# Keys and gates of a gated delta layer from the input without its norm factor

## Chip, core and metric

One core of a Trainium2 chip runs the whole program. The metric is the device time of one execution in microseconds (us); less is better. The kernel before took 1216.96 us, the median of three runs (1216.34 to 1221.76).

## What is computed

Two transformer blocks in a row on 256 tokens of 1024 features, in float32. The first layer is a gated delta layer; the change lies at its entrance:

```python
def rmsnorm(x, w):
    xf = x.astype(jnp.float32)
    y = xf * lax.rsqrt(jnp.mean(xf * xf, axis=-1, keepdims=True) + EPS)
    return (y * w.astype(jnp.float32)).astype(x.dtype)
...
def gated_deltanet(hn, w_in, conv_w, a_log, dt_bias, out_norm_w, w_out):
    proj = hn @ w_in
    qkv, z, b, a = jnp.split(proj, [...], axis=-1)
    qkv = jax.nn.silu(causal_dwconv(qkv, conv_w))
    q, k, v = jnp.split(qkv, [GDN_QK_DIM, 2 * GDN_QK_DIM], axis=-1)
    ...
    beta = jax.nn.sigmoid(b)
    g = -jnp.exp(a_log) * jax.nn.softplus(a + dt_bias)
    o = chunked_gated_delta_rule(q, k, v, g, beta)
    ...
```

`hn` is `rmsnorm(h, a_norm_w)`. The factor of the norm is one number for each token, the weight one for each feature, so a product with `w_in` may be taken of `h * weight` and each token's factor put on the result. q and k are then made to unit length for each head; behind this layer come its feed-forward, an attention layer, and a second block, none of which the change touches.

## The kernel before

Features lie on the 128 partitions and tokens on the free dimension: `h` is 8 tiles of 128x256. All weights come in one stream of tiles `wr` of 512 KB (128x1024, eight blocks of 128x128) in the order of use, issued on SP's queue (`_raw`, L172), four buffers deep. Each is split in two (`_prep`): ScalarE makes a rounded copy `wh` (L186), VectorE the difference `wl` (L187); each has four buffers, so a copy waits until TensorE is done with the tile four before. An input is split the same way into `xh` and `xl`, and `mm3` takes three products: `wh` with `xh`, `wh` with `xl`, `wl` with `xh` (L249 to L251). In what follows a product is one such matmul of 128x128 by 128x256, and a k-step is one of the 8 feature tiles.

`gdn` starts with warm-up products on ones (`warm`), while `h` lands in four pieces. ScalarE squares, VectorE adds the squares (`add_sq`, L502), TensorE sums over the partitions (`colsum`), a chain of short VectorE instructions makes the factor (`rstd`), and `rows` brings it into row form (a diagonal `dg` and a product with ones, `rowp`). For each k-step VectorE makes `xn` (L568), ScalarE `xh` (L569), VectorE `xl` (L570).

`gdn_body` then takes the products of `w_in`: keys (four groups of two tiles, 48 products each, the first two groups together with k outside), the gates b and a (24 products), queries (four groups), z, values. What becomes of a finished group is its evacuation: for keys and queries `conv`, which is one scaled copy on ScalarE (`cy`, L647) and three steps on VectorE (L650) for each of two tiles, then silu on ScalarE (L651) and a square (`sqg`); for the gates `evac_ba`, some fifteen short instructions on VectorE and five on ScalarE. The column sums of `sqg` (`ssb`, four products with ones, 8 records) and the gates' transposition (`bgp`) are queued some ticks later: a tick comes with every four weight blocks, that is 12 products, and steps the waiting generators (`side`). Behind the keys follow `x_stage` (kk, rp), an inverse of triangular blocks in 31 steps on VectorE (`inv_stage`), and the rest of the layer.

The program's order on each engine is set by a scheduler when it is built; each engine then works off its own queue in order. Tiles named `t2` share six buffers. `behind` fixes that one instruction stands after another without a wait.

Of the kernel before, what the change touches and what calls it, by code (L numbers as in the profile page):

```python
# [9 lines left out]
F32 = mybir.dt.float32  # L10
# [9 lines left out]
P = 128  # L20
T = 256
# [91 lines left out]
WARM = (5, 1, 3)  # L113
# [19 lines left out]
PRE0 = 1  # L133
# [5 lines left out]
PINS = {1: 0, 3: 1}  # L139
# [3 lines left out]
class Builder:  # L143
# [113 lines left out]
    def gemm(self, name, x, K, ctiles, evac, ko=0):  # L257
# [3 lines left out]
        if ko:  # L261
            banks = [self.bank() for _ in range(ko)]
            for k in range(K):
                for g in range(ko):
                    for i, c in enumerate(groups[g]):
                        wh, wl = self.w(name, k * P, c * P)
                        self.mm3(banks[g][:, i * T : i * T + T], wh, wl, xh[:, k], xl[:, k],
                                 k == 0 and i == 0, k == K - 1, True)
# [159 lines left out]
    def split(self, hi, lo, src, scale=None, eng=None):  # L428

        nc = self.nc  # L430
        if scale is None:
            nc.scalar.activation(hi, src, AF.Copy)
            nc.vector.tensor_tensor(lo, src, hi.bitcast(F32), ALU.subtract)
# [71 lines left out]
    def run(self):  # L505
        nc, tc = self.nc, self.tc
        with ExitStack() as es:
# [9 lines left out]
            self.ident = self.cp.tile([P, P], F32, name="ident")  # L517
            for b in range(4):
# [4 lines left out]
            self.ones = self.cp.tile([P, P], F32, name="ones")  # L523
            nc.gpsimd.memset(self.ones, 1.0)
# [22 lines left out]
    def gdn(self):  # L547
# [3 lines left out]
        with tc.tile_pool(name="gp", bufs=1) as gp:  # L551

            wb = self.bank("warm")
            warm = lambda n, r: [nc.tensor.matmul(wb[:, 0 : r.shape[1]], self.ones, r, start=True, stop=True) for _ in range(n)]
            warm(WARM[0], self.ones)
            for b in range(4):
                self.add_sq(self.sqs, "sqa", b, lambda o: nc.scalar.activation(o, self.h[:, 2 * b : 2 * b + 2], AF.Square))
            nc.vector.tensor_tensor(self.sqs[0], self.sqs[0], self.sqs[1], ALU.add)
            cs = self.colsum(self.sqs[:1])
            if PRE0:  # L560
                self._prep(0)
            rc = self.rstd(cs, D)
            warm(WARM[1], self.sqs[0])
            rb = self.rows(rc, psum=True)
            warm(WARM[2], self.h[:, 0])
            for i in range(8):
                t = gp.tile([P, T], F32, tag="t2", bufs=6, name="xn")
                op = nc.vector.scalar_tensor_tensor(t, self.h[:, i], self.col("a_norm", i), rb, ALU.mult, ALU.mult)  # L568
                nc.scalar.activation(x[0][:, i], t, AF.Copy)  # L569
# [1366 lines left out]
```

## Time and profile before

| what | value |
|---|---|
| median of the runs shown | 1216.96 us |
| the profiled execution | 1216.23 us |
| its span | 1214.4 us |
| TensorE (PE) busy | 1188.7 us, 98% |
| VectorE (DVE) busy | 895.2 us, 74% |
| ScalarE (ACT) busy | 687.7 us, 57% |
| GpSimd (POOL) busy | 20.4 us, 2% |
| DMA over the span | 168 GB/s read and written |

The span is the time between the first and last instruction of the profiled execution; 1.8 us lie around it. Busy shares are averages over all stages. A busy TensorE is one with products in its pipeline: products overlap, so the distance from one start to the next says what one costs. A timeline row gives the start, the length, engine, line, operation, tile and count; "idle before" in brackets is the time that the engine stood still, and what ended it. Where one row merges several instructions, its length reaches from the first start to the last end.

### The profile page before, as it was taken

The numbers are of one execution on the slowest core, as the hardware profiler recorded it, in microseconds if no ns is written. First come the engines' busy times: TensorE is split into PE (matmuls) and PEld (weight loads), VectorE is DVE, ScalarE is ACT, GpSimd is POOL, SyncE is SP. The second block draws the span as 40 slices with busy tenths as digits, with TensorE's granted clock in tenths as the row PEclk, the third lists the DMA queues.
The fourth block names the chain that finished last, engine by engine and source line by source line (L and its number), as shares of the span: only waits on it lengthen the run. The fifth ranks groups of instructions, "written<-read, shape, count | busy, mean of one in ns | idle before, by whom it ended". The sixth has DMA issues, their size and how long they took to land.

```text
span 1214.4 us, 23416 instructions
## 1 busy us (share of the span) xinstructions
PE 1188.7 (98%) x9368; PEld 1125.4 (93%) x9368; DVE 895.2 (74%) x1680; ACT 687.7 (57%) x1170; POOL 20.4 (2%) x47
## 2 busy tenths in 40 slices
PE   7999989999999999999999999999999999999997
PEld 6989878999999999889999999889789999999996
DVE  6978976668877778878977778756756567655555
ACT  5785547546655556656755556754465445444443
POOL 1000000000000000000000000000000000000000
PEclk9999999999999999999999999999999999999999
DMA  6546365355555557435555564364255563555552
GB/s 222 179 132 216 125 192 183 124 157 168 199 184 182 187 179 243 126 115 161 190 188 183 187 191 158 112 207 134 87 161 173 188 234 118 186 179 187 189 179 83
DMA packets 68318, 206.01 MB, mean 170 GB/s; under 512 B 18198, under 2 KB 18342, under 8 KB 67953
## 3 DMA queue, kind: packets, MB, share of 16 engines
q1 hardware_dynamic: 65600, 194.77, 50.3%
q0 software_dynamic: 2608, 9.75, 2.2%
q8 instruction: 73, 1.20, 0.4%
q14 instruction: 37, 0.29, 0.1%
HBM read 199.75 MB, written 4.74 MB: 168 GB/s over the span
## 4 chain that ended last, share of the span: by engine, by line
PE 92%; DVE 4%; ACT 2%; DMA 1%; issue 1%; SPq 0%; DVEq 0%; ACTq 0%
PE pb L249 21%; PE pb L250 20%; PE pb L251 20%; PE acc L249 7%; PE acc L250 7%; PE acc L251 7%; DVE wl L187 1%; PE pt L1138 1%; PE ssb L669 1%; DMA wr<-wall 0%; DMA h<-xT 0%; PE z2p L855 0%; PE y2p L847 0%; PE kv L1542 0%; PE csum L366 0%
## 5 line engine op out<-in xcount | busy, mean ns | idle before, releaser
L187 DVE TENSOR_TENSOR wl<-wr,wh 128x1024 fp32r<-128x1024 f32 x362 | 441.5, 1223 | 193.7 <-ACT wh L186 192.3
L186 ACT ACTIVATE wh<-wr 128x1024 fp32r<-128x1024 f32 x362 | 381.6, 1057 | 338.3 <-issue 101.1
L251 PE MATMUL pb<-xh,wl 128*128 128x256 f32 x1224 | 345.6, 283 | 3.9 <-DVE wl L187 3.9
L249 PE MATMUL pb<-xh,wh 128*128 128x256 f32 x1224 | 347.8, 284 | 0.6 <-ACT xh L569 0.6
L250 PE MATMUL pb<-xl,wh 128*128 128x256 f32 x1224 | 345.5, 282 | 0.2 <-DVE xl L570 0.2
L249 PEld LDWEIGHTS pb<-xh,wh 128*128 128x128 f32 x1224 | 231.7, 189 | 2.8 <-issue 1.3
L251 PEld LDWEIGHTS pb<-xh,wl 128*128 128x128 f32 x1224 | 229.7, 188 | 4.5 <-DVE wl L187 4.5
L250 PEld LDWEIGHTS pb<-xl,wh 128*128 128x128 f32 x1224 | 230.1, 188 | 0.5 <-DVE xl L570 0.4
L249 PE MATMUL pb<-fh,wh 128*128 128x256 f32 x416 | 118.3, 285 | 0.0
L250 PE MATMUL pb<-fl,wh 128*128 128x256 f32 x416 | 117.5, 283 | 0.1
L251 PE MATMUL pb<-fh,wl 128*128 128x256 f32 x416 | 116.6, 281 | 0.0
L249 PE MATMUL acc<-ah,wh 128*128 128x256 f32 x352 | 98.7, 280 | 0.0
L251 PE MATMUL acc<-ah,wl 128*128 128x256 f32 x352 | 98.5, 280 | 0.0
L250 PE MATMUL acc<-al,wh 128*128 128x256 f32 x352 | 98.5, 280 | 0.0
L249 PEld LDWEIGHTS pb<-fh,wh 128*128 128x128 f32 x416 | 77.9, 188 | 1.4 <-issue 0.4
L250 PEld LDWEIGHTS pb<-fl,wh 128*128 128x128 f32 x416 | 78.1, 188 | 1.1 <-DVE fl L436 0.3
L251 PEld LDWEIGHTS pb<-fh,wl 128*128 128x128 f32 x416 | 78.9, 190 | 0.0
L977 DVE SCALAR_TENSOR_TENSOR fy<-fpad,cols,fy 128x256 f32<-128x256 f32 x176 | 73.6, 478 | 0.0
L249 PE MATMUL pb<-wh,xh 128*128 128x512 f32 (+1 forms) x176 | 70.5, 402 | 0.0
L250 PE MATMUL pb<-wl,xh 128*128 128x512 f32 (+1 forms) x176 | 68.1, 387 | 0.5 <-DVE wl L187 0.5
L251 PE MATMUL pb<-wh,xl 128*128 128x512 f32 (+1 forms) x176 | 68.0, 387 | 0.0
L249 PEld LDWEIGHTS acc<-ah,wh 128*128 128x128 f32 x352 | 66.9, 190 | 0.0
(437 smaller groups left out, 2091.2 us busy)
## 6 DMA issues: line engine op xcount, KB each, us to landing
wr<-wall SPq DMA_DIRECT2D x362, 512.0 KB, 3.6
wzd<-zt POOLq DMA_DIRECT2D x8, 256.0 KB, 3.0
wzog<-wzd POOLq DMA_DIRECT2D x4, 512.0 KB, 5.2
bias<-bd POOLq DMA_DIRECT2D x4, 512.0 KB, 7.7
h<-xT SPq DMA_DIRECT2D x4, 256.0 KB, 4.0
h<-xT POOLq DMA_DIRECT2D x1, 1024.0 KB, 5.9
wrow<-wrow POOLq DMA_DIRECT2D x1, 1024.0 KB, 10.0
out_dram<-mw SPq DMA_DIRECT2D x4, 256.0 KB, 2.0
```

The source lines that it names most:

```text
L186: nc.scalar.activation(hi, r, AF.Copy)
L187: i = nc.vector.tensor_tensor(lo, r, hi.bitcast(F32), ALU.subtract)
L249: mm(out, ah, bh, start=start, stop=False, skip_group_check=skip)
L250: mm(out, ah, bl, start=False, stop=False, skip_group_check=skip)
L251: mm(out, al, bh, start=False, stop=stop, skip_group_check=skip)
L669: nc.tensor.matmul(ssb[:, c : c + 1], sq[:, i, tt * P : tt * P + P], self.ones[:, 0:1], start=True, stop=True)
L977: nc.vector.scalar_tensor_tensor(y[:, i], u[:, i, j : j + T], w(j), y[:, i], ALU.mult, ALU.add)
L1138: nc.tensor.transpose(pt[:, j * P : j * P + P], S[:, i, j * P : j * P + P], self.ident)
```

## The change

Raw input: `rawtile` makes `rawh` (ScalarE, `h` times the norm's weight) and `rawl` (VectorE) for each k-step, without the factor. Keys and gates take their products of these; each key group is multiplied by the factor's row form in a new step `ku` (VectorE, out of PSUM) before its convolution, and the gates in one of 48x256. Queries, z and values still take normed x, which is now made in a generator (`norm`): GpSimd multiplies `ha` (`h` times the weight, made by GpSimd too) by the row form, ScalarE rounds, GpSimd makes the difference. GpSimd adds the squares; the column sum is queued 7 ticks in, the row form 4 ticks after it, and is copied to SBUF (`rowb`). SP's queue takes pieces of `h` and weight tiles by turns, `ident` goes to GpSimd's queue, and the norm's weight (`anw`) has a small DMA of its own on ScalarE's. The warm-up is 13 products. The first two key groups' products come in three runs for each k-step. The gates' transposition waits nine ticks, not six. Two small products of weights for the last block (`wfp`, `w1f`) are put behind the last split of the feed-forward.

```diff
-WARM = (5, 1, 3)
+WARM = 13
+NA1, NA2 = 7, 4
...
@@ gemm, the first ko groups
+                for o, wh, wl, first in ts:
+                    mm(o, wh, xh[:, k], start=first, stop=False, skip_group_check=True)
+                for o, wh, wl, first in ts:
+                    mm(o, wh, xl[:, k], start=False, stop=False, skip_group_check=True)
+                for o, wh, wl, first in ts:
+                    mm(o, wl, xh[:, k], start=False, stop=k == K - 1, skip_group_check=True)
...
@@ run
+            nc.scalar.dma_start(self.anw, self.a["cols"][:, 0:KD])
             for b in range(4):
                 nc.sync.dma_start(self.h[:, 2 * b : 2 * b + 2], self.a["xT"][:, 2 * b : 2 * b + 2])
-            nc.sync.dma_start(self.ident, self.cst("ident"))
-            self._raw(0)
+                if b < 3:
+                    self._raw(b)
+            nc.gpsimd.dma_start(self.ident, self.cst("ident"))
             nc.sync.dma_start(self.cols, self.a["cols"])
...
@@ gdn
+            def rawtile(i):
+                act.append(nc.scalar.activation(raw[0][:, i], self.h[:, i], AF.Copy, scale=self.anw[:, i : i + 1]))
+                dve.append(nc.vector.scalar_tensor_tensor(raw[1][:, i], self.h[:, i], self.anw[:, i : i + 1], raw[0][:, i].bitcast(F32), ALU.mult, ALU.subtract))
...
+            nc.gpsimd.tensor_tensor(s0, s0, s1_, ALU.add)
...
+            nc.gpsimd.tensor_tensor(s0, s0, s2_, ALU.add)
...
+            fold = nc.gpsimd.tensor_tensor(s0[:, 0], s0[:, 0], s0[:, 1], ALU.add)
+            dve.append(nc.vector.tensor_tensor(s3_[:, 0], s3_[:, 0], s3_[:, 1], ALU.add))
...
+            def norm():
+                for _ in range(NA1):
+                    yield
+                rc = self.rstd(self.colsum([s0[:, 0], s3_[:, 0]]), D)
+                for _ in range(NA2):
+                    yield
+                self.rb = self.rows(rc)
+                self.ready = True
+                self.flush()
+                for i in range(8):
+                    t = gp.tile([P, T], F32, tag="t2", bufs=6, name="xn")
+                    nc.gpsimd.tensor_tensor(t, self.ha[i], self.rb, ALU.mult)
+                    nc.scalar.activation(x[0][:, i], t, AF.Copy)
+                    nc.gpsimd.tensor_tensor(x[1][:, i], t, x[0][:, i].bitcast(F32), ALU.subtract)
+                    yield
...
@@ evac_ba
+            nc.vector.tensor_tensor(e1[A], b[A, :T], self.rb[A], ALU.mult)
...
             def later():
-                for _ in range(6):
+                for _ in range(9):
                     yield
...
@@ mk_evac
+                if key == "kss":
+                    u = t2([P, 2, T], "ku")
+                    nc.vector.tensor_tensor(u, ev2(b), self.bc2(self.rb), ALU.mult)
+                    b = u.rearrange("p a t -> p (a t)")
                 conv(b, ct0 + 2 * g, d)
...
-        gk = self.gemm("w_in", x, KD, list(range(8, 16)), mk_evac(kT, 0, 8, "kss"), ko=2)
+        gk = self.gemm("w_in", raw, KD, list(range(8, 16)), mk_evac(kT, 0, 8, "kss"), ko=2)
         next(gk)
-        list(self.gemm("w_ba", x, KD, [0], evac_ba))
+        list(self.gemm("w_ba", raw, KD, [0], evac_ba))
```

Three places of the order. ScalarE from the last copies of x to the first key group, before (L569 makes `xh`, L186 a weight copy `wh`, L647 the convolution's first step `cy`, L613 to L617 are the gates):

```order
L569 ACTIVATE xh<-xn 128x256 x3
L186 ACTIVATE wh_306<-wr_244 128x1024
L186 ACTIVATE wh_349<-wr_274 128x1024
L647 ACTIVATE cy<-pb,cols 128x256
L186 ACTIVATE wh_410<-wr_304 128x1024
L186 ACTIVATE wh_440<-wr_347 128x1024
L647 ACTIVATE cy<-pb,cols 128x256
L613 ACTIVATE gcr<-gr 16x256
L615 ACTIVATE gr<-gr 48x256
L647 ACTIVATE cy<-pb,cols 128x256
L617 ACT_TABLE_LOAD
L617 ACTIVATE gr<-gr 48x256
```

ScalarE from the end of the first key group's convolution to the first copies `xh` in the changed kernel (L185 is the weight copy, L714 is `cy`, L718 silu, L680 to L684 the gates, L732 the square, L630 makes `xh`):

```order
L718 ACT_TABLE_LOAD
L718 ACTIVATE kT<-cy 128x512
L680 ACTIVATE gcr<-gr 16x256
L732 ACTIVATE sqg<-kT 128x512
L682 ACT_TABLE_LOAD
L682 ACTIVATE gr<-gr 48x256
L714 ACTIVATE cy<-ku,cols 128x256
L684 ACT_TABLE_LOAD
L684 ACTIVATE gr<-gr 48x256
L714 ACTIVATE cy<-ku,cols 128x256
L630 ACTIVATE xh<-xn 128x256 x2
L185 ACTIVATE wh_602<-wr_509 128x1024
```

All copies of x stood ahead of the first `cy` before; now the first key group with its silu and square, all of the gates, the second group's `cy` and three table loads stand ahead of the first `xh`.

GpSimd from its last memset of the start to its cast of the mask, before:

```order
L1009 MEMSET w1f 128x16
L589 CAST identb<-ident 128x128
L584 DMA mask_186<-cst 128x384
L767 MEMSET h 32x32x32
L588 CAST mask3b<-mask_186 128x384
```

and in the changed kernel, to the first differences `xl` (L602 to L610 add squares, L638 makes `ha`, L629 `xn`, L631 `xl`):

```order
L1080 MEMSET w1f 128x16
L655 CAST identb<-ident 128x128
L602 ISA
L602 TENSOR_TENSOR sq<-sq 128x512
L605 TENSOR_TENSOR sq<-sq 128x512
L610 TENSOR_TENSOR sq<-sq 128x256
L638 TENSOR_TENSOR ha<-h,anw 128x256 x8
L650 DMA mask_172<-cst 128x384
L838 MEMSET h 32x32x32
L654 CAST mask3b<-mask_172 128x384
L629 TENSOR_TENSOR xn<-ha,rowb 128x256 x2
L631 TENSOR_TENSOR xl<-xn,xh 128x256 x2
```

Eleven instructions on two inputs each, with an ISA instruction in front, stand ahead of the mask, and `xn` and `xl`, which were VectorE's, behind it.

TensorE in the changed kernel, from the queries' second k-step on, with the gates' transposition (L702) and an `ssb` (L740); `wh_511` and `wh_602` are the first and the third weight tile of the queries:

```order
L248 MATMUL pb<-xh,wh_511 128x256
L249 MATMUL pb<-xl,wh_511 128x256
L250 MATMUL pb<-xh,wl_512 128x256
L248 MATMUL pb<-xh,wh_511 128x256
L702 MATMUL bgp<-ident,stk 128x80 x2
L249 MATMUL pb<-xl,wh_511 128x256
L250 MATMUL pb<-xh,wl_512 128x256
L248 MATMUL pb<-xh,wh_602 128x256
L249 MATMUL pb<-xl,wh_602 128x256
L250 MATMUL pb<-xh,wl_603 128x256
L248 MATMUL pb<-xh,wh_602 128x256
L249 MATMUL pb<-xl,wh_602 128x256
```

Before, the queries' first tile was done as a whole, and the second after it; now the first tile stops behind its third k-step, and the first three k-steps of the second tile stand in between.

## Rows read from the trace of the kernel before

**Rows 1.** The page's first part: busy time, share of the span, instructions.

```profile
PE 1188.7 (98%) x9368; PEld 1125.4 (93%) x9368; DVE 895.2 (74%) x1680; ACT 687.7 (57%) x1170; POOL 20.4 (2%) x47
```

**Rows 2.** Stretches: length, busy time (instructions) of each engine, clock, DMA share, GB/s.

```profile
15.00:30.00 15.00, 14.11 (x113) 13.71 (x114) 12.48 (x21) 7.62 (x13) 2.25 (x3) 1.00 0.52 172
...
120.00:160.00 40.00, 37.50 (x258) 33.97 (x256) 39.63 (x100) 22.01 (x37) 0.00 (x0) 1.00 0.49 150
160.00:200.00 40.00, 37.22 (x447) 33.29 (x448) 24.96 (x51) 21.96 (x45) 2.14 (x4) 1.00 0.62 198
```

**Rows 3.** TensorE in time: start, length, what [idle before].

```profile
0.99 2.50 PE L554 MATMUL warm<-ones 128*128 128x128 f32 x10 [0.99 <-POOL ones L524]
9.29 1.01 PE L366 MATMUL csum<-ones,sqa 128*128 128x1 f32 x4 [5.80 <-DVE sqa L558]
...
13.26 0.74 PE L418 MATMUL rowp<-dg,ones 128*128 128x128 f32 x4 [0.19 <-DVE dg L416]
...
15.02 0.50 PE L249 MATMUL pb<-xh,wh 128*128 128x256 f32 x2 [0.59 <-ACT xh L569]
...
42.12 0.29 PE L251 MATMUL pb<-xh,wl 128*128 128x256 f32 x1
42.24 0.95 PE L669 MATMUL ssb<-ones,sqg 128*128 128x1 f32 x8
43.05 0.36 PE L249 MATMUL pb<-xh,wh 128*128 128x256 f32 x1
...
56.80 0.39 PE L249 MATMUL pb<-wh,xh 128*128 128x512 f32 x1
```

**Rows 4.** ScalarE in time, the first 13 us.

```profile
4.11 0.63 ACT L557 ACTIVATE sqa<-h 128x512 f32<-128x512 f32 x1 [2.10 <-DMA h<-xT]
...
8.43 1.06 ACT L186 ACTIVATE wh<-wr 128x1024 fp32r<-128x1024 f32 x1 [1.23 <-DMA wr<-wall]
...
10.45 1.06 ACT L186 ACTIVATE wh<-wr 128x1024 fp32r<-128x1024 f32 x1 [0.74 <-DMA wr<-wall]
11.73 1.06 ACT L186 ACTIVATE wh<-wr 128x1024 fp32r<-128x1024 f32 x1 [0.23 <-DMA wr<-wall]
```

**Rows 5.** ScalarE in time, the first key group.

```profile
34.13 1.28 ACT L617 ACT_TABLE_LOAD   x1
...
38.11 0.63 ACT L651 ACTIVATE kT<-cy 128x512 f32<-128x512 f32 x1
38.65 0.45 ACT L647 ACTIVATE cy<-pb,cols 128x256 f32<-128x256 f32 x1
39.00 0.62 ACT L661 ACTIVATE sqg<-kT 128x512 f32<-128x512 f32 x1
```

**Rows 6.** VectorE in time, gates and convolution.

```profile
32.33 0.53 DVE L611 TENSOR_SCALAR gr<-pb,cols 48x256 f32<-48x256 f32 x1
...
36.13 0.40 DVE L618 SCALAR_TENSOR_TENSOR gr<-gr 48x256 f32<-48x256 f32 x1
...
40.89 0.55 DVE L626 TENSOR_TENSOR gch<-gcr,gch 16x384 fp32r<-16x384 f32 x1
41.47 2.43 DVE L650 SCALAR_TENSOR_TENSOR cy<-pb,cols,cy 128x255 f32<-128x255 f32 x6
```

**Rows 7.** VectorE by form (280 to 400 us); two of its lines, ns min/median/max; GpSimd's cast.

```profile
L970 DVE TENSOR_TENSOR fpad<-pb,rowb 128x512 f32<-128x512 f32 x15 | 10.2, 688 | 4.6 <-PE pb L251 4.6
...
L570 DVE TENSOR_TENSOR xl<-xn,xh x8: 412/416/721, 15.2 to 21.0; 128x256 fp32r<-128x256 f32 x8
...
L187 DVE TENSOR_TENSOR wl<-wr,wh x362: 1202/1225/1520, 10.7 to 1198.2; 128x1024 fp32r<-128x1024 f32 x181
...
21.08 0.66 POOL L588 CAST mask3b<-mask 128x384 bf16<-128x384 f32 x1
```

**Rows 8.** TensorE's last product, and the stretch of the end.

```profile
1206.46 0.39 PE L251 MATMUL acc<-wh,al 128*128 128x512 f32 x1
...
1212.00:1214.00 2.00, 0.00 (x0) 0.00 (x0) 0.00 (x0) 0.00 (x0) 0.00 (x0) 0.50 0.37 142
```

More of the change, by code (lines that the diff above doesn't have):

```diff
@@ L132 @@
 PTD = (1, 3)
-PRE0 = 1
 NX = 2
@@ L138 @@
 QS = "sgss"
-PINS = {1: 0, 3: 1}
 ORDER = "qqzqqzvvvvvvzvvz"
@@ L553, in gdn @@
             wb = self.bank("warm")
[L554 to L561, printed above, removed]
@@ L574, in gdn @@
-            self.gdn_body(gp, x)
-    def gdn_body(self, gp, x):
+            for _ in range(WARM):
+                nc.tensor.matmul(wb[:, 0:P], self.ones, self.ones, start=True, stop=True)
+            raw = (gp.tile([P, KD, T], F32R, tag="XA", name="rawh"), gp.tile([P, KD, T], F32R, tag="EA", name="rawl"))
+            act, dve = [], []
+            act.append(nc.scalar.activation(self.sp.tile([P, 2], F32, tag="rky", bufs=2, name="tl"), self.ones[:, 0:2], AF.Square))
+            def rawtile(i):
+                act.append(nc.scalar.activation(raw[0][:, i], self.h[:, i], AF.Copy, scale=self.anw[:, i : i + 1]))
+                dve.append(nc.vector.scalar_tensor_tensor(raw[1][:, i], self.h[:, i], self.anw[:, i : i + 1], raw[0][:, i].bitcast(F32), ALU.mult, ALU.subtract))
@@ new lines, in part, with square @@
+            def part(j, s):
+                r, hi, lo = self.raws0[j], *self.halves[j]
+                act.append(nc.scalar.activation(hi[:, s], r[:, s], AF.Copy))
+                dve.append(nc.vector.tensor_tensor(lo[:, s], r[:, s], hi[:, s].bitcast(F32), ALU.subtract))
+            def square(b):
+                t = gp.tile([P, 2, T], F32, tag="t2", bufs=6, name="sq")
+                act.append(nc.scalar.activation(t, self.h[:, 2 * b : 2 * b + 2], AF.Square))
+                return t
+            self.raws0 = {}
@@ new lines, in gdn @@
+            for j in range(3):
+                self.raws0[j] = self.raws.pop(j)
+                self.raws[j] = None
+                self.halves[j] = (self.wtile(j, F32R, "wh"), self.wtile(j, F32R, "wl"))
+            lo, hi, full = slice(0, 512), slice(512, 1024), slice(0, 1024)
+            rawtile(0)
+            part(0, lo)
+            rawtile(1)
+            part(0, hi)
+            rawtile(2)
+            rawtile(3)
+            part(1, full)
+            s0 = square(0)
+            rawtile(4)
@@ new lines, in gdn @@
+            rawtile(5)
+            s1_ = square(1)
+            self._raw(3)
+            nc.gpsimd.tensor_tensor(s0, s0, s1_, ALU.add)
+            part(2, full)
+            s2_ = square(2)
+            nc.gpsimd.tensor_tensor(s0, s0, s2_, ALU.add)
+            rawtile(6)
+            rawtile(7)
+            s3_ = square(3)
+            self._raw(4)
+            fold = nc.gpsimd.tensor_tensor(s0[:, 0], s0[:, 0], s0[:, 1], ALU.add)
+            dve.append(nc.vector.tensor_tensor(s3_[:, 0], s3_[:, 0], s3_[:, 1], ALU.add))
@@ new lines, in gdn @@
+            for l in (act, dve):
+                for p, n in zip(l, l[1:]):
+                    self.behind(n, p)
+            self.dvl = dve[-1]
+            self.ready = False
+            def norm():
[13 more added lines that the diff above has]
+                    yield
@@ L577, in gdn_body @@
+            hab = gp.tile([P, KD, T], F32, tag="vn", name="ha")
+            self.ha = [hab[:, i] for i in range(8)]
+            for i in range(8):
+                self.behind(nc.gpsimd.tensor_tensor(self.ha[i], self.h[:, i], self.anw[:, i : i + 1].to_broadcast([P, T]), ALU.mult), fold)
+            self.side(norm())
+            self.gdn_body(gp, x, raw)
+    def gdn_body(self, gp, x, raw):
         nc, tc, sp = self.nc, self.tc, self.sp
@@ L589, in gdn_body @@
         nc.gpsimd.tensor_copy(identb, self.ident)
-        nc.vector.tensor_tensor(identr, self.ident[:, 32:48], self.ident[:, 64:80], ALU.add)
+        self.behind(nc.vector.tensor_tensor(identr, self.ident[:, 32:48], self.ident[:, 64:80], ALU.add), self.dvl)
         stk = gp.tile([P, T], F32, tag="stk", name="stk")
```

30 lines of the change are left out of this document (10 added, 20 removed).

## Prediction

> **What bounds the kernel now.** I read the page's first part, then the stretches, then TensorE in order of time. The first part says who is the limit: TensorE is busy 1188.7 of 1214.4 us, VectorE comes next with 74% [rows 1]. A saving is worth only what it lets TensorE start earlier or not wait. The stretches say where it waits: 0.89 us in 15 to 30, 2.5 in 120 to 160, where VectorE is busy 39.63 of 40, 2.8 in 160 to 200 [rows 2]. TensorE's own rows show the largest hole: the first real product stands at 15.02 us; ahead of it are only warm-up products, the column sum and the row form [rows 3]. From there a product of 256 columns follows the last after 0.12 us (42.12 to 42.24). My landmark is the first product of z, 56.80 us. Ahead of it stand 312 products of keys, gates and two groups of queries (counted in the order; the same 312 in both programs), three groups of ssb (0.81 us each, 42.24 to 43.05) and the gates' transposition: 15.02 + 312 x 0.12 + 3 x 0.81 + 0.2 = 55.1 us, and 1.7 us of waits. What the change gives must be seen there.
>
> **The start.** The raw products need one piece of h and half a weight tile. h's first piece landed at 4.11 us. The first tile is now second on SP's queue, not sixth; tiles of 512 KB that were waited for came 1.28 us apart (10.45, 11.73), so it lands at 5.4 to 5.8; its half is copied in 0.63 us, as a Square of 512 columns [rows 4]. TensorE could start at 6.2. The 13 warm-up products are 26 records, where 10 took 2.50 us: at that pace they end at 7.5, at rowp's (4 in 0.74) at 5.8 [rows 3]. I take 6.5 and keep 6.2 and 7.5. ScalarE and VectorE now scale h, split the first tiles and square in turn; from their queues TensorE waits about 0.5 us in the first four tiles. The second square is done at about 11.2 (second tile copied by 9.4, then two squares and two scalings), the fourth tile's copy at 15.3.
>
> Into TensorE's stream come the column sum (8 records as in ssb, 0.81) and the row form (0.74) [rows 3]. Had nothing else to wait, z would start at 6.5 + 37.4 + 2.6 + 0.8 + 0.7 + 0.5 = 48.5: **8.3 us earlier.**
>
> **What is late next: x for the queries.** They still take normed x, and its making starts behind the row form, 141 products in. Before, the factor took from 10.30 (end of the column sum) to 13.26 with one weight difference inside [rows 3]; now three are inside, 5.4 us from 17.9: ready in time. The row form ends at 6.5 + 16.9 + 0.8 + 0.5 + 0.7 = 25.4, and TensorE reaches the first product with x 75 products later, at 34.4. ScalarE's queue (the order above) puts all of the first key group and of the gates ahead of the first xh. Start to start:
> - rowb 0.4: 25.9. VectorE: ku 0.69 (as the feed-forward's product with rowb), the gates' product 0.53, a weight difference 1.23, six convolution steps 2.43 [rows 6, 7]: 30.7.
> - ScalarE waits for that: table load 1.28, kT 0.54, tanh 0.4, sqg 0.6, table load 1.28, exponential 0.4, cy 0.36, table load 1.28, logarithm 0.4, cy 0.36 (the short ones priced as cy) [rows 5]: 37.5. The first xh ends at 37.9. TensorE has waited **3.5 us**.
> - VectorE waits for the logarithm (37.1), then makes the gates' rows. Before, these took from 36.13 to 41.44, first to last, with one weight difference and two convolution steps among them [rows 6]; with four steps and no difference it is 4.9 us: 42.0. Then ku, a step, and the difference that the second query tile needs: 44.3, some 2.5 us after TensorE has used the three k-steps of x that it had.
> - ScalarE again: table load, kT, cy, sqg from 43.1: 45.9; only then xh 3 to 6, at 0.36 each. GpSimd makes each one's xl. No row has a GpSimd instruction with two inputs; the nearest is the cast of 128x384 in 0.66 us [rows 7], 1.7 ns an element: 0.44 for 256 elements, 0.88 for the 512 read. I take the middle, 0.66. The four end at 48.9. Then 11 products of the second tile, ssb and the eighth k-step: 51.3; 51 products are left, 6.1 us. Two halves of a step overlap with the products, 0.3: z starts at **57.1, against 56.80.** The 8.3 us are used up on one chain through ScalarE and VectorE.
>
> **VectorE and GpSimd.** GpSimd was busy 20.4 us in all [rows 1]; it gets 11 instructions early (two of 512 columns), 16 later. Does that cost VectorE? The rows say yes: the cast (21.08 to 21.74) fell on an xl of 0.721 where the median is 0.416 and on a weight difference of 1.520 where it is 1.225: 0.6 us lost for 0.66 [rows 7]. Early, 13 x 0.66 = 8.6 us from 11.2 on lie over the difference of the fourth tile, which is due at 16.6 (80 products): I count 1.0 us of TensorE's waiting. Later, five instructions, 3.3 us, fall on the gates' rows: I count 1.5. Each could be 0, were VectorE idle or elsewhere.
>
> GpSimd's first sum has an ISA instruction in front that the old order lacks there. It has no row; the nearest load is a table's 1.28 us [rows 5], and I allow 0 to four times that. It can start at some 6.5 us, when ident is cast; until 11.2 the squares hide it, and 2 us more the slack of the sum, which is due at 17.1. I take 0. The GPSIMD Engine Reference of the Trainium skill (Instruction dispatch) gives about 6 us for the first call after a load; by it the sum stays as it is.
>
> **At nothing.** ident goes to GpSimd's queue and cols behind three tiles on SP's; the first reader of ident is GpSimd's cast, and cols stands ahead of the fourth tile, which is needed later than the third. The gates' transposition stands 22 products later in TensorE's order; its reader, the keys' factors, waits for the last ssb anyway. The products of the first two key groups in three runs a k-step: the same count. wfp and w1f behind the last split: two short instructions in a stretch where VectorE isn't the limit; ahead of the boundary they would cost under 0.5. 16 xn and xl leave VectorE, 8 raw differences and 4 ku come: ahead of z it is a limit only on the chain above. After z's start TensorE's order is the old one, so its offset there is carried to the end; VectorE has then one convolution (2.43) more before it, which is free if it is idle for so long before the inverse begins, and otherwise lies in the range.
>
> **The sum.** +0.3 + 1.0 + 1.5 = +2.8 us on the profiled execution's 1216.23: **1219.0**. The median of the runs shown is 0.73 above that execution; I leave the number there. With each step's bounds (start -0.3 and +1.0, GpSimd's price -1 and +2.5, the chain's other terms -2 and +2, both contentions 0): 1213 to 1224.
>
> **Rivals.**
> - *x in time (faster).* If the chain to xh is shorter than I add up, TensorE keeps the 8.3 us less the early contention: 1216.2 - 8.3 + 1.0 = 1209. It is decided at TensorE's first query product: from there a k-step of x must come every 1.4 us. For it: I add every step at its full price. Against it: three table loads stand ahead of xh, in an order that is fixed. 0.19.
> - *VectorE and GpSimd exclude each other (slower).* If each instruction of the one with two inputs in SBUF waits for a whole one of the other, they go in turn. The fourth weight difference, which has three other differences, a sum and identr ahead of it, then starts at 19.1, not 15.3, and ends at 20.3: 3.7 us of TensorE's time. Later, five xn and xl on the gates' rows cost 3.3, and three xl that each stand behind a weight difference or convolution steps 3: 0.3 + 3.7 + 6.3 = +10.3, **1226**. For it: 0.6 lost of 0.66. Against: many of VectorE's instructions there have one input, or one in PSUM. It decides once the fourth difference starts after 17 us. 0.28. The page SBUF — State Buffer of the Trainium skill (SBUF: two separate sides) says just this for two SBUF inputs against a GpSimd instruction that reads SBUF, "an exclusive lock, not a bandwidth split"; the cast's row agrees, but no row has long runs of both.
> - *The start isn't early.* If SP's pieces land together and not in turn, the first tile lands as before (copied from 8.43 on [rows 4]) and products start at 9.2: +2.7, 1222. The 1.28 us speak against it. 0.04, within no change.
> - TensorE's clock: it ended at 1206.85, and the granted clock read 0.50, the lower level, in 1212 to 1214 [rows 8]. In 34 to 51 us TensorE works less than half the time. At the lower level the last 51 products would take 6.1 us more at most; I take 0 and put 3 into the range.
>
> **How the numbers follow.** 0.5%, 6.1 us, is about what a measurement of this kernel can tell from no change: faster is below 1210.9, slower above 1223.0. Forecast 0.49 (its own range 1213 to 1224), late start 0.04, x in time 0.19, exclusion 0.28. So faster 0.19, no change 0.53, slower 0.28. The range takes in most of both sides: 1210 to 1229.
>
> **What will show it.** Right: the first raw product at 6.2 to 7.5 us; a wait of TensorE for ScalarE's xh at about 34, another for a weight difference some 8 us later; z's first product at 57 to 60. x in time would put that at 49 to 51. Exclusion would show as GpSimd rows of 128x256 over 1 us, weight differences over 1.6, and over 2 us of waiting for the fourth. I am wrong if z starts early and the end doesn't follow, or if TensorE waits in 120 to 200 us for much more than the 5.3 us of before.

## The result, and the profile after

The changed kernel takes 1226.65 us (median of 5 runs, 1226.09 to 1228.79), the kernel before 1218.74 in the runs taken with it: a ratio of 1.0077, 95% interval 1.0062 to 1.0092. It is 0.8% slower, by 7.9 us in the medians and by 10.0 in the two profiled executions (1226.25 against 1216.23). The forecast was 1219.0, with a range to 1229.

First the page's first part (before: [rows 1]). GpSimd's 28.8 us more have not made VectorE idler: it is busy 9.0 us longer, and ScalarE 6.4.

```profile
PE 1196.2 (98%) x9380; PEld 1132.2 (92%) x9380; DVE 904.2 (74%) x1675; ACT 694.1 (57%) x1183; POOL 49.2 (4%) x75
```

TensorE in order of time (before: [rows 3]; start, length, in brackets the idle time before and what ended it).

```profile
0.99 5.24 PE L564 MATMUL warm<-ones 128*128 128x128 f32 x26 [0.99 <-POOL ones L525]
6.81 0.74 PE L270 MATMUL pb<-rawh,wh 128*128 128x256 f32 x4 [0.58 <-ACT wh L576]
...
18.49 0.74 PE L274 MATMUL pb<-rawh,wl 128*128 128x256 f32 x4 [1.58 <-DVE wl L186]
...
36.27 0.28 PE L250 MATMUL pb<-rawh,wl 128*128 128x256 f32 x1
39.98 0.58 PE L248 MATMUL pb<-xh,wh 128*128 128x256 f32 x1 [3.44 <-ACT xh L630]
40.36 1.70 PE L740 MATMUL ssb<-ones,sqg 128*128 128x1 f32 x8
...
44.78 0.50 PE L702 MATMUL bgp<-ident,stk 80*128 80x80 f32 x2 [1.23 <-issue]
...
48.75 0.58 PE L250 MATMUL pb<-xh,wl 128*128 128x256 f32 x1 [2.53 <-DVE wl L186]
...
58.28 0.48 PE L248 MATMUL pb<-xh,wh 128*128 128x256 f32 x2
58.74 0.39 PE L249 MATMUL pb<-xl,wh 128*128 128x256 f32 x1
...
65.08 0.39 PE L248 MATMUL pb<-wh,xh 128*128 128x512 f32 x1
...
172.45 0.24 PE L894 MATMUL y1p<-h,XA 32*32 32x32 f32 x2
```

The last of these rows in the kernel before:

```profile
164.35 0.24 PE L823 MATMUL y1p<-h,XA 32*32 32x32 f32 x2
```

The raw products start 8.2 us earlier, the first product of z 8.3 later. Between them TensorE waits 1.6 for the fourth weight difference, 3.4 for the first xh, 1.2 for the gates' transposition, 2.5 for a weight difference of the queries. From z on the offset is carried: 8.10 at the first product of the inverse's stage (y1p, 172.45 against 164.35), 10.09 at the last product (1216.55 against 1206.46, [rows 8]).

ScalarE's queue shows where x stands (before: [rows 5]).

```profile
27.58 0.38 ACT L428 ACTIVATE rowb<-rowp 128x256 f32<-128x256 f32 x1 [1.56 <-PE rowp L424]
...
39.53 0.71 ACT L630 ACTIVATE xh<-xn 128x256 fp32r<-128x256 f32 x2
...
47.20 0.51 ACT L714 ACTIVATE cy<-ku,cols 128x256 f32<-128x256 f32 x1 [3.46 <-DVE ku L728]
47.73 1.28 ACT L718 ACT_TABLE_LOAD   x1
...
50.48 1.32 ACT L630 ACTIVATE xh<-xn 128x256 fp32r<-128x256 f32 x4
54.87 0.51 ACT L714 ACTIVATE cy<-ku,cols 128x256 f32<-128x256 f32 x1 [3.07 <-DVE ku L728]
...
57.22 0.40 ACT L630 ACTIVATE xh<-xn 128x256 fp32r<-128x256 f32 x1
```

Four xh stand behind the second key group, the eighth behind the third, and the third and the fourth key group each begin with a wait for VectorE's ku. The last xl ends at 58.69. TensorE takes it up at 58.74, after a wait of some 0.2 us, and z follows 6.4 us after the xl, the time of the products that still stand ahead of it.

VectorE beside GpSimd, by form (28 to 62 us; in all, mean ns of one, idle before), and GpSimd's two groups:

```profile
L717 DVE SCALAR_TENSOR_TENSOR cy<-ku,cols,cy 128x253 f32<-128x253 f32 x8 | 5.5, 695 | 0.1
L717 DVE SCALAR_TENSOR_TENSOR cy<-ku,cols,cy 128x255 f32<-128x255 f32 x8 | 4.7, 598 | 1.8 <-ACT cy L714 1.8
L717 DVE SCALAR_TENSOR_TENSOR cy<-ku,cols,cy 128x254 f32<-128x254 f32 x8 | 4.7, 595 | 0.1
...
L691 DVE COPY gcr<-gcr 16x128 f32<-16x128 f32 x1 | 0.8, 768 | 0.0
...
L629 POOL TENSOR_TENSOR xn<-ha,rowb 128x256 f32<-128x256 f32 x8 | 9.4, 1175 | 7.1 <-DVE cy L717 4.8 <-DVE gch L693 1.8 <-ACT kT L718 0.5
L631 POOL TENSOR_TENSOR xl<-xn,xh 128x256 fp32r<-128x256 f32 x8 | 6.7, 857 | 7.2 <-ACT xh L630 7.2
```

One of the same rows in the kernel before (14 to 58 us):

```profile
L650 DVE SCALAR_TENSOR_TENSOR cy<-pb,cols,cy 128x255 f32<-128x255 f32 x10 | 4.7, 474 | 0.4 <-ACT cy L647 0.3
```

The 24 convolution steps of the keys take 14.9 us, each counted at its own length; at the 0.47 of before they would take 11.3. Last, stretches (length, busy time and instructions of each engine, granted clock): TensorE's clock falls to 0.50, the lower level, while it waits.

```profile
36.00:42.00 6.00, 2.56 (x15) 2.35 (x13) 3.13 (x6) 5.14 (x9) 1.99 (x3) 0.79 0.12 47
42.00:54.00 12.00, 8.22 (x36) 7.37 (x36) 11.84 (x18) 5.93 (x11) 8.59 (x10) 0.50 0.27 86
54.00:58.00 4.00, 4.00 (x24) 3.76 (x23) 3.96 (x9) 2.36 (x5) 1.75 (x3) 0.68 0.02 6
```

### The profile page after: what moved, and what is told of

It is laid out like the page before. It is cut to its first block, busy times and chain, and to the rows that moved or that the text cites. A ratio compares the mean times of both kernels' runs of the same rounds, so it can differ in the third digit from the quotient of the medians.

```text
span 1224.5 us, 23491 instructions
## 1 busy us (share of the span) xinstructions
PE 1196.2 (98%) x9380; PEld 1132.2 (92%) x9380; DVE 904.2 (74%) x1675; ACT 694.1 (57%) x1183; POOL 49.2 (4%) x75
## 4 chain that ended last, share of the span: by engine, by line
PE 88%; DVE 7%; ACT 3%; issue 1%; DMA 0%; DVEq 0%; SPq 0%; ACTq 0%
PE pb L248 19%; PE pb L249 19%; PE pb L250 18%; PE acc L248 7%; PE acc L249 7%; PE acc L250 7%; DVE wl L186 2%; DVE cy L717 1%; PE pb L274 1%; PE pb L270 1%; PE pb L272 1%; PE ssb L740 1%; DMA wr<-wall 0%; ACT wh L185 0%; PE z2p L926 0%
## 5 line engine op out<-in xcount | busy, mean ns | idle before, releaser
L186 DVE TENSOR_TENSOR wl<-wr,wh 128x1024 fp32r<-128x1024 f32 x359 | 438.8, 1225 | 190.3 <-ACT wh L185 188.8
L185 ACT ACTIVATE wh<-wr 128x1024 fp32r<-128x1024 f32 x359 | 378.9, 1057 | 332.0 <-issue 97.5
L250 PE MATMUL pb<-xh,wl 128*128 128x256 f32 x1072 | 305.7, 285 | 5.6 <-DVE wl L186 5.6
L248 PE MATMUL pb<-xh,wh 128*128 128x256 f32 x1072 | 307.1, 287 | 3.4 <-ACT xh L630 3.4
L249 PE MATMUL pb<-xl,wh 128*128 128x256 f32 x1072 | 305.3, 285 | 0.0
L248 PEld LDWEIGHTS pb<-xh,wh 128*128 128x128 f32 x1072 | 205.4, 192 | 5.4 <-ACT xh L630 3.6
L250 PEld LDWEIGHTS pb<-xh,wl 128*128 128x128 f32 x1072 | 203.7, 190 | 6.4 <-DVE wl L186 6.3
L249 PEld LDWEIGHTS pb<-xl,wh 128*128 128x128 f32 x1072 | 204.1, 190 | 0.4 <-POOL xl L631 0.2
```

Of the source, the lines that this page charges most:

```text
L185: nc.scalar.activation(hi, r, AF.Copy)
L186: i = nc.vector.tensor_tensor(lo, r, hi.bitcast(F32), ALU.subtract)
L248: mm(out, ah, bh, start=start, stop=False, skip_group_check=skip)
L249: mm(out, ah, bl, start=False, stop=False, skip_group_check=skip)
L250: mm(out, al, bh, start=False, stop=stop, skip_group_check=skip)
```

## The experiments

Each edit is made to the changed kernel. Ratios are to the kernel before on the same chip. Theory A: VectorE and GpSimd get in each other's way, and that is the loss. B: TensorE's lower clock is. C: x comes late in ScalarE's order. D and E, from the first runs: the end is set by VectorE's work behind the row form, whatever TensorE does.

### GpSimd's late half of x on VectorE (e1_late_v)

```diff
-nc.gpsimd.tensor_tensor(t, self.ha[i], self.rb, ALU.mult)
+nc.vector.tensor_tensor(t, self.ha[i], self.rb, ALU.mult)
-nc.gpsimd.tensor_tensor(x[1][:, i], t, x[0][:, i].bitcast(F32), ALU.subtract)
+nc.vector.tensor_tensor(x[1][:, i], t, x[0][:, i].bitcast(F32), ALU.subtract)
```

> The sixteen xn and xl of the changed kernel are made on VectorE instead of GpSimd, in the same place of the program, nothing else. Theory A (VectorE and GpSimd get in each other's way, and that is most of the loss): GpSimd's rows of 0.73 to 0.99 us become VectorE rows of 0.42, the convolution steps beside them go back from 0.48-0.59 to 0.41, the gates' rows take 5 us rather than 6.8, the last xl ends at about 54 rather than at 57.7, z starts at about 62 rather than 65.1: 1223.5. Theory C (the order in which ScalarE takes keys, gates and x is what holds TensorE, whoever makes x): x comes when ScalarE's queue lets it, z stays at 64 to 66: 1225 to 1228. Theory B (TensorE's lower clock is the loss): no change, 1226.5.

Measured: 1227.35, ratio 1.0079 (1.0066 to 1.0092), z at 66.29. VectorE, the same view:

```profile
L717 DVE SCALAR_TENSOR_TENSOR cy<-ku,cols,cy 128x255 f32<-128x255 f32 x8 | 3.6, 478 | 1.7 <-ACT cy L714 1.7
...
L631 DVE TENSOR_TENSOR xl<-xn,xh 128x256 fp32r<-128x256 f32 x8 | 3.2, 418 | 0.5 <-ACT xh L630 0.5
L629 DVE TENSOR_TENSOR xn<-ha,rowb 128x256 f32<-128x256 f32 x8 | 3.0, 414 | 0.0
...
L691 DVE COPY gcr<-gcr 16x128 f32<-16x128 f32 x1 | 0.2, 217 | 0.0
```

The rows do what theory A says: a convolution step goes from 0.60 to 0.70 back to 0.48, the copy from 0.77 to 0.22. In all 4.1 us come back on the 24 steps (14.9 to 10.8) and 2.4 on six stretched instructions of the gates: 6.5. But the sixteen instructions cost VectorE 6.2. It is a swap at par, and theory A's 1223.5 is a miss. The last xl ends at 58.57, where it ended at 58.69. That z is 1.2 later even so is TensorE's: from 52.5 to 59.6 it has no wait, but its clock reads 0.50 and a product comes every 0.21 us.

### h times anw on ScalarE (e2_ha_act)

```diff
-self.behind(nc.gpsimd.tensor_tensor(self.ha[i], self.h[:, i], self.anw[:, i : i + 1].to_broadcast([P, T]), ALU.mult), fold)
+self.behind(nc.scalar.activation(self.ha[i], self.h[:, i], AF.Copy, scale=self.anw[:, i : i + 1]), self.whs[3 + n])
```

(two of the eight behind each of the fourth to seventh weight copies)

> The eight products h times anw are made on ScalarE behind the weight copies instead of on GpSimd, so GpSimd runs only the three sums early; late xn and xl stay on GpSimd. Theory A: the fourth weight difference starts at 15.5 rather than 17.2 and takes 1.23, TensorE's wait for it (1.6) goes, the last raw product stands at about 34.5 rather than 36.3, rowb at 25.7 rather than 27.6, and everything behind it is 2 us earlier: z at 63, 1224.5. Theory C: the same 1.6 to 2 us, as only the early part is touched, but the wait for xh stays at 3.4. Theory B: z within 0.5 of 65.1, 1226.5.

Measured: 1224.89, ratio 1.0067 (1.0048 to 1.0085). TensorE's wait for the fourth difference is 0.73, not 1.58, rowb starts at 26.59, not 27.58; the wait for xh is still 3.43, z is at 64.53. The early contention is worth 1.0 us at the row form; its effect on the whole time is within the intervals.

### Idle products in the waits (e3_warm)

```diff
+FILL = {(0, 0, 0): 15, (0, 0, 2): 8, (0, 0, 3): 12}
...
+        for _ in range(n):
+            i = self.nc.tensor.matmul(o, self.ones, self.ones, start=True, stop=True, skip_group_check=True)
```

(numbers of idle products ahead of the first, third and fourth k-step of the first query group; some fall on sums already open in that bank, so the queries' values change, the instructions don't)

> 35 idle products of 128x128 are put into TensorE's order where it waits (15 ahead of the first query product, 8 ahead of the third k-step, 12 ahead of the fourth), written to columns that a later product overwrites. The granted clock should then stay near 1.0 from 36 to 54 us, where it fell to 0.50. Theory B (the clock is the loss): the last 48 query products and the ssb groups run at 0.12 and 0.9 us rather than 0.21 and 1.7, z starts 3 to 4 us earlier, at 61.5: 1223. Theories A and C: the last xl comes at 57.7 all the same, z stays within 0.8 of 65.1: 1226 to 1227.

Measured: 1226.50, ratio 1.0072 (1.0059 to 1.0085). The same stretches as above:

```profile
36.00:42.00 6.00, 5.36 (x42) 4.77 (x42) 3.20 (x6) 5.08 (x9) 2.06 (x3) 1.00 0.07 27
42.00:54.00 12.00, 9.87 (x76) 9.08 (x74) 11.84 (x18) 5.93 (x11) 8.60 (x10) 0.93 0.27 88
54.00:58.00 4.00, 4.00 (x19) 3.85 (x19) 3.96 (x9) 2.37 (x5) 1.75 (x3) 0.50 0.01 5
```

and the product that corresponds to the one at 58.28 above:

```profile
59.50 0.49 PE L258 MATMUL pb<-xh,wh 128*128 128x256 f32 x2
```

The clock is up at 1.00 and 0.93 until 54, and z stands at 66.06, 0.2 beyond what A and C allowed and not earlier; the last xl ends at 58.63, as without. As z needs 6.4 us from the last xl on, no clock could have brought it ahead of 65.0 here: as the cause of this kernel's late z, theory B falls. But the run does not show that the lower clock is free. From 52.5 on products come every 0.21 us again, after another wait of 1.5 us for sqg, and TensorE reaches the eighth k-step only 0.9 us after its xl has landed. In the changed kernel it was there some 0.2 us ahead of it. So x and the clock hold z at nearly the same time, and a version that brings x earlier meets the clock next.

### x ahead of keys and gates, on VectorE (e6_xfirst_v)

```diff
-                self.ready = True
-                self.flush()
                 for i in range(8):
...
-                    nc.gpsimd.tensor_tensor(t, self.ha[i], self.rb, ALU.mult)
+                    nc.vector.scalar_tensor_tensor(t, self.h[:, i], self.anw[:, i : i + 1], self.rb, ALU.mult, ALU.mult)
...
-                    nc.gpsimd.tensor_tensor(x[1][:, i], t, x[0][:, i].bitcast(F32), ALU.subtract)
-                    yield
+                    nc.vector.tensor_tensor(x[1][:, i], t, x[0][:, i].bitcast(F32), ALU.subtract)
+                self.ready = True
+                self.flush()
...
-                self.behind(nc.gpsimd.tensor_tensor(self.ha[i], self.h[:, i], self.anw[:, i : i + 1].to_broadcast([P, T]), ALU.mult), fold)
```

> x comes first: the evacuations of keys and gates are held until all eight k-steps of x are queued, and xn and xl are made on VectorE straight from h, anw and the row form (no ha, nothing late on GpSimd). Theory C (the order on ScalarE): rowb at 26 to 27.6, then 16 VectorE instructions of 0.42: the last xl by 35, before TensorE ends the raw products at 34.5 to 36.4; no wait for xh; z at 36.4 + 96 x 0.12 + 2.6 + 0.3 = 50.8 if the keys' late evacuation holds nothing, 53 if it costs a wait of 2: 1212 to 1215, faster than before by 3 to 6. Theory A: only what the two engines cost each other comes back, 1.6 early and 3 late: z at 60, 1222. Theory B: whatever shortens the waits keeps the clock up; it adds at most the 3 to 4 of the idle-product run to either.

Measured: 1224.14, ratio 1.0059 (1.0040 to 1.0077). TensorE:

```profile
47.99 0.50 PE L697 MATMUL bgp<-ident,stk 80*128 80x80 f32 x2 [5.68 <-issue]
...
57.40 0.40 PE L248 MATMUL pb<-wh,xh 128*128 128x512 f32 x1
```

No wait for x at all, as theory C has it; but the gates, now behind x, make TensorE wait 5.7 us for their transposition, and from 48 to 54 its clock reads 0.51. Theory C's z (50.8 to 53) and time (1212 to 1215) are misses. z comes 0.6 later than before, and y1p 7.4 later (171.80; the profiled execution took 1227.22, and its clock read 0.96 from 120 to 160 us, so that part of the 7.4 may be the execution's). So z was no landmark for the end any more: theories D and E.

### x for free (e5_x_free)

```diff
-raw = (gp.tile([P, KD, T], F32R, tag="XA", name="rawh"), gp.tile([P, KD, T], F32R, tag="EA", name="rawl"))
+raw = x
...
-                    nc.gpsimd.tensor_tensor(t, self.ha[i], self.rb, ALU.mult)
-                    nc.scalar.activation(x[0][:, i], t, AF.Copy)
-                    nc.gpsimd.tensor_tensor(x[1][:, i], t, x[0][:, i].bitcast(F32), ALU.subtract)
...
-                self.behind(nc.gpsimd.tensor_tensor(self.ha[i], self.h[:, i], self.anw[:, i : i + 1].to_broadcast([P, T]), ALU.mult), fold)
```

> Queries, values and z take the raw halves too: norm factor, xn, xh and xl are left out altogether, so the output lacks the factor there. It prices the chain that makes x. Theory C (x comes late on ScalarE and VectorE, and z starts 6.4 after the last xl): no wait for xh; TensorE next waits for the gates' transposition, which is 2 to 4 earlier without x in the queues: z at 52 to 56, 1214 to 1217. Theory D (the end is set behind z, by VectorE's queue up to the end of the inverse; in the x-first run z was 0.6 late and the end 11): z early, but y1p no earlier than 170 and the end at 1222 or more.

Measured: 1218.85 (10 runs, 1214.49 to 1223.04), ratio 1.0001 (0.9984 to 1.0018). (Some products of z now stand ahead of queries, so z is no mark here.) TensorE waits 2.7 us at the first row form of the gates (46.38), until VectorE's ku; y1p is at 165.61, 1.3 behind the kernel before, in a profiled execution of 1222.99. Making x (ha with it) costs the change all of its loss, and without it the 8.2 us of early start still buy nothing. Both theories miss: the time lies between C's 1214 to 1217 and D's 1222, and y1p does not stand at D's 170. Where the early start goes is in the trace. First the stretch from the end of rowb to the first product of the keys' decay, and one of TensorE behind its waits (third busy time: VectorE; then the clock):

```profile
26.96:71.61 44.65, 41.53 (x267) 38.70 (x265) 34.16 (x80) 33.07 (x52) 0.00 (x0) 0.89 0.37 125
```

```profile
48.90:57.80 8.90, 8.90 (x42) 8.90 (x43) 7.35 (x13) 2.59 (x4) 0.00 (x0) 0.50 0.70 233
```

and VectorE's longest waits in the first:

```profile
56.57 1.23 DVE L186 TENSOR_TENSOR wl<-wr,wh 128x1024 fp32r<-128x1024 f32 x1 [1.55 <-ACT wh L185]
60.78 2.43 DVE L706 SCALAR_TENSOR_TENSOR cy<-pb,cols,cy 128x255 f32<-128x255 f32 x6 [2.98 <-ACT cy L703]
66.33 1.23 DVE L186 TENSOR_TENSOR wl<-wr,wh 128x1024 fp32r<-128x1024 f32 x1 [1.81 <-ACT wh L185]
```

VectorE is busy 34 of 44.7 us here and stands idle for 6.3 between 54.9 and 66.3, so its work is not what bounds this stretch. TensorE waits 3.1 (2.7, then 0.4 for sqg) and then runs without a wait at the lower clock, where 35 products come every 0.21 us and not every 0.12 and an ssb takes 1.56 and not 0.81: by these rows I estimate 4 us. The two are 7 of the 8.2. A run with x for free and the clock kept up was not made, so what the early start would then be worth stays open.

### x first, and the transposition later (e9_xfirst_gates_late)

```diff
 (the run with x first, and)
-                for _ in range(9):
+                for _ in range(24):
```

> The x-first run with one number more: the gates' transposition is queued 24 ticks behind the gates instead of 9, so 328 products stand ahead of it, not 264, and it lies just behind the start of z. Theory C: the wait of 5.7 for it goes, TensorE reaches z at 51 to 52 without a wait: 5 earlier than before. If TensorE's early start carried through, the end would be at 1212 to 1214. Theory D: the keys' factors and the inverse come no earlier for it, the wait moves behind z (the keys' products and row forms wait for gates and keys), y1p at 170 to 172 as in the x-first run: 1222 to 1225.

Measured: 1230.20, ratio 1.0094 (1.0078 to 1.0110).

```profile
47.99 0.39 PE L248 MATMUL pb<-wh,xh 128*128 128x512 f32 x1
...
182.96 0.24 PE L889 MATMUL y1p<-h,XA 32*32 32x32 f32 x2
```

z starts 8.8 us **earlier** than before, and the inverse's first product 18.6 **later**. The transposition, queued behind 328 products, comes only at 58.93, and VectorE copies its result at 75.31, behind four weight differences; the keys' decay comes at 81.40. It isn't the only thing that is late: TensorE also waits 3.5 us for sqg, and its clock reads 0.50 from 54 to 62 and 0.65 from 62 to 70. Neither theory's time holds (D's 1222 to 1225 is a miss too). An early z alone is worth nothing here.

### The row form early (e7_row_early, e8_row_early_ha)

```diff
-NA1, NA2 = 7, 4
+NA1, NA2 = 6, 1
```

(both; in the second h times anw is on ScalarE too, behind the fifth weight copy)

> Two numbers only: the column sum one tick and the row form four ticks earlier in TensorE's order (72 and 96 products ahead of them instead of 84 and 141). Theory C: rowb is made at 22 to 23 rather than 27.6 (the factor, 2.6 us of VectorE plus two weight differences behind the column sum, is the limit), the whole chain of keys, gates and x moves with it, last xl at 53.5, z at 60: 1221 to 1222. Theory D: z at 60 as well, but as VectorE has the same work up to the inverse, y1p comes 1 to 2 earlier at most: 1224 to 1225. Theory A (the two engines in each other's way): sums and ha now lie beside the factor's instructions, rowb not before 25, z at 62 or later: 1224.

> The row form early as in the run above, and h times anw on ScalarE instead of GpSimd. Theory C: rowb at 21 to 22, the fourth weight difference not held (raw phase ends at 35 rather than 36.4), the xh stand between keys and gates in ScalarE's order: z at 56 to 58, the clock stays up for more of it: 1216 to 1219, level with before. Theory D: z at 56 to 58, end at 1222 or more.

Measured: 1230.83, ratio 1.0098 (1.0084 to 1.0113), and 1227.56, ratio 1.0070 (1.0057 to 1.0084). The row form in the first and in the second:

```profile
25.62 1.23 PE L424 MATMUL rowp<-dg,ones 128*128 128x128 f32 x4 [4.99 <-DVE dg L422]
```

```profile
21.84 0.71 PE L425 MATMUL rowp<-dg,ones 128*128 128x128 f32 x4 [1.64 <-DVE dg L423]
```

With ha on GpSimd the factor is not made sooner, and TensorE waits 5.0 for it (theory A's 25, at z 69.57); without, the row form is 3.8 earlier. Even so z is only at 64.47: x, now earlier on GpSimd, falls on the keys' convolution, whose first six steps take 3.91 where they take 2.45 in the run with x first. The first run's expected times were all too low; of the second's only theory D's "1222 or more" holds.

### The row form early, nothing late on GpSimd (e10_row_early_v)

```diff
-NA1, NA2 = 7, 4
+NA1, NA2 = 6, 2
```

(with xn and xl on VectorE as in the run with x first, in their old place, and no ha)

> Nothing late on GpSimd and no ha: xn and xl on VectorE from h, anw and the row form, x in its old place between the keys; column sum one tick and row form three ticks earlier in TensorE's order (72 and 120 products ahead). Theory E (VectorE's work behind the row form sets when the keys' products and the inverse can start: 43.2 us from rowb to the first product with the keys' decay in the x-first run, whoever waits): rowb at 24, that product at 67 to 68 (before 65.0, changed kernel 75.2), z and everything behind it 2 to 4 later than before: 1220 to 1222, between the two kernels. Theory C (x alone): z at 57 or earlier, level with before or 2 faster, 1215 to 1218.

Measured: 1226.06 (1223.61 to 1228.82, the lowest is the profiled execution), ratio 1.0067 (1.0053 to 1.0082). z is at 61.48, y1p at 171.08. The stretch from the end of rowb to the first product of the keys' decay, for the kernel before (from its row form), the changed one, x first, and this one (third busy time: VectorE):

```profile
14.00:64.98 50.98, 49.53 (x384) 47.12 (x384) 46.04 (x98) 34.17 (x58) 2.25 (x3) 1.00 0.53 175
```

```profile
27.96:75.18 47.22, 40.01 (x247) 36.73 (x246) 40.57 (x80) 33.44 (x57) 16.47 (x17) 0.82 0.37 119
```

```profile
26.92:70.37 43.45, 37.77 (x256) 35.27 (x255) 39.70 (x95) 34.70 (x58) 0.94 (x1) 0.88 0.37 119
```

```profile
24.07:70.02 45.95, 40.22 (x260) 37.18 (x259) 40.30 (x97) 33.07 (x54) 0.94 (x1) 0.85 0.37 129
```

VectorE is busy some 40 us in these three forms of the change, 86 to 91% of the stretch, and the keys' decay is not reached in under 43. With the row form at 24 it comes 5 us later than before, at 70.02, not at the 67 to 68 expected, and theory E's 1220 to 1222 is a miss, as is C's time. The run with x for free, where VectorE is busy for 34 us only, does not reach the decay sooner either (44.65). None of these versions beats the kernel before.

### What of GpSimd slows VectorE (e11_pool_memset, e11_pool_copy, e11_pool_tt)

```diff
 (the run with the row form early and ha on ScalarE, and in ha's place on GpSimd, eight times)
+nc.gpsimd.memset(dz[:, 0:4], 0.0)
 (or)
+nc.gpsimd.tensor_copy(dz[:, i], self.h[:, i])
 (or)
+nc.gpsimd.tensor_tensor(dz[:, i], self.h[:, i], self.anw[:, i : i + 1].to_broadcast([P, T]), ALU.mult)
```

> The run with the row form early and ha on ScalarE, plus eight idle memsets of 128x1024 on GpSimd in the place where the changed kernel makes ha: GpSimd is as busy, but reads nothing. There the row form waited 1.6 us and stood at 21.8 without, and waited 5.0 and stood at 25.6 with ha on GpSimd. Theory A1 (what hurts is that GpSimd reads SBUF): row form at 21.8 to 22.2, the factor's instructions and weight differences as without (1.22). Theory A2 (any instruction of GpSimd hurts): 24 to 26.

> The same with eight idle copies of 128x256 out of h on GpSimd: one input in SBUF. Theory A1: the copies hurt as ha does, in proportion to their time: each instruction of VectorE may wait for one copy, row form at 23.5 to 26. Theory A3 (only instructions with two inputs hurt): 21.8 to 22.2.

> The same with eight idle products of h and anw on GpSimd, the instruction of the changed kernel, its result not used: the control. Theories A1 to A3 all expect the row form at 25 to 26 with a wait of 4 to 5 us of TensorE for it. If it stands at 22, what cost time in the run with the row form early was not GpSimd but the order of the weight differences.

One execution each. The row form stands at 22.96 (a wait of 2.7), 22.85 (2.3) and 24.58 (3.9), without them at 21.84 (1.6): GpSimd is what costs. None of the three lands where a theory put it: the memsets between A1's 22.2 and A2's 24, the copies between A3's 22.2 and A1's 23.5, the products ahead of 25. VectorE beside the memsets:

```profile
20.04 0.28 DVE L361 SCALAR_TENSOR_TENSOR rky<-rkt,rky 128x1 f32<-128x1 f32 x2
...
20.37 1.22 DVE L187 TENSOR_TENSOR wl<-wr,wh 128x1024 fp32r<-128x1024 f32 x1
...
21.83 1.14 DVE L423 TENSOR_SCALAR dg<-ident,rd 128x128 f32<-128x128 f32 x2
```

and beside the products of two inputs:

```profile
21.65 0.65 DVE L361 SCALAR_TENSOR_TENSOR rky<-rkt,rky 128x1 f32<-128x1 f32 x2
...
22.79 1.21 DVE L187 TENSOR_TENSOR wl<-wr,wh 128x1024 fp32r<-128x1024 f32 x1
```

Beside products the two short instructions with two inputs take 0.65, beside copies 0.42, beside memsets 0.28, as alone. The memsets instead stretch the one-input dg: 1.14 for two, 0.48 without. So none of the theories A1 to A3 holds as stated: it goes by the pair of instructions. SBUF — State Buffer of the Trainium skill (SBUF: two separate sides) has both halves: an exclusive lock that a VectorE instruction needs either for two SBUF inputs, then only against a GpSimd instruction that reads SBUF, or in a mode that uses both ports, whatever GpSimd does. The rows of two inputs agree with the first half; those of dg agree with the second if dg runs in such a mode, which no run here shows.

## Why the prediction was right or wrong

**The time: inside the range, but not by the forecast.** The median, 1226.65, lies outside the forecast's own 1213 to 1224. The stated range, 1210 to 1229, holds it only because it was drawn to take in the rival at 1226, and that rival's mechanism is not what happened: that part is luck.

**The start: right.** Raw products at 6.81 (6.5 was taken), 8.2 us early. GpSimd's ISA instruction cost nothing that the trace shows: the first sum starts at 11.36, right behind the second square.

**x late behind keys and gates: right in kind.** The waits came as put down: 3.44 for xh (3.5), 2.53 for a weight difference 8.8 us later (2.5, some 8 later). Removing x (ha with it) brings the time back to that of the kernel before.

**The chain's sizes: wrong.** Forecast and measured, in us: rowb done at 25.9, 27.96; first xh done at 37.9, 39.9; gates' rows done at 42.0, 46.05; the four xl done at 48.9, 54.76; z at 57.1, 65.08. It loses four times about 2 us, 8.0 in all, of which the sum's two contention terms (1.0 and 1.5) had provided 2.5, for a z at 59.6. The first 2 come before rowb: TensorE waited 1.58 for the fourth difference, not 1.0, though ha itself accounts for only 1.0 of them (the run with ha on ScalarE). The second and third are the step "I count 1.5": the gates' rows took 6.8, not 4.9 (4.6 in the run without GpSimd's late half), an xl 0.86, not 0.66, and the keys' convolution, which the sum took at its old length, lost most. In all VectorE's instructions grew by 6.5 us. The fourth is the step "the eighth k-step: 51.3": the eighth xh stands behind the third key group in ScalarE's queue, at 57.22, a place that the program's order fixes and the sum left out. The lower clock alone would have cost nearly as much there: TensorE came to that k-step, at a product every 0.21 us, some 0.2 us ahead of its xl.

**Exclusion, the rival at 1226:** its point of decision came true (the fourth difference started at 17.22), and its time. Of its signs, GpSimd's rows over 1 us came for xn (1.18 in the mean) and ha (1.01), not for xl (0.86); of the weight differences one reached 1.63 (at 18.4), the others took 1.21 to 1.47, and TensorE's wait for the fourth was 1.58, not over 2. Its early price, 3.7, was under 2, and its later one, 6.3 of TensorE's time, can't be set beside the 6.5 by which VectorE's instructions grew. That price would have come back with the work on VectorE, and it did not: VectorE pays 6.2 for the work itself, and z was no earlier. GpSimd beside VectorE added next to nothing to what the two do together in this stretch.

**The clock: 0 came true, by little.** It fell to 0.50 for 12 us and more, and x came only 0.2 us after TensorE had reached it. With x earlier the clock would have had a price, as in the run with x for free (some 4 us, the estimate above); the 3 us in the range were well put.

**After z: right** that the offset is carried (8.28 at z, 8.10 at y1p), and that 120 to 200 us wait no more than before (5.1 against 5.3). Of the 10.09 at the end, 1.5 arise between 182 and 190 us; from 180 to 190 this execution's clock read 0.83 and that of before 1.00; from y2p's first product to z2p's it is 8.2 us here and 6.7 before, and 6.7 in the profiles of the first three experiments as well, so it belongs to the execution and not to the change. Why the clock falls there in some executions was not tried.

**What no step of it said:** the early start did not pay in any version. The row form ends at 14.0 before [rows 3], rowb at 27.96 after, and everything that needs the factor, some 40 us of VectorE's time with the weight differences between, begins 14 us later, while TensorE is only 8 us ahead. With x first, z was level with before and the keys' decay 5.4 later (70.37), with VectorE busy for 91% of the stretch: that fits VectorE's work behind the row form as the next bound. The run with x for free does not fit it. VectorE had some 6 us less to do there than in the changed kernel and was busy for 77%, and still the decay was 6.6 later (71.61) than before; y1p was only 1.3 later, so the decay does not set the end by itself. There the rows show TensorE's waits and its lower clock in the place of the early start. Which of the two, VectorE's work or the clock behind the waits, would hold a better version is not shown.

## What to carry to other kernels

When a change lets the bound engine start early by putting off a factor, count the work of the other engines that waits for the factor, and the time that is left for it; and ask what the bound engine's clock does when it has to wait behind its early start. Work moved from VectorE to GpSimd is no relief where both run at once: price it at the VectorE time that it takes away, here 6.5 us for 6.2. And follow every consumer on the in-order queues to the last one: the eighth of eight came last of all, behind a key group.

## What was not expected of the hardware

It is the short instructions that pay most. Beside GpSimd's products a weight difference mostly keeps its length (1.21 at 20.97 and 23.74, but 1.47 at 12.25 and 1.63 at 18.4), while an instruction of 0.22 takes 0.53, and a copy of 16x128 takes 0.77 for 0.22. The 0.3 to 0.6 us more look like a wait for the rest of a GpSimd instruction before they start; no run here shows that by itself. On GpSimd the same xl takes 0.86 (0.73 to 0.99), on VectorE 0.42; the GPSIMD Engine Reference of the Trainium skill (Engine selection) has about twice for two inputs, and these rows agree. The rows of xn, 1.18 against 0.41, are nearer three times.
